# Interleaving two tensors on one core: uniform tile widths and an early output write that is copied from the input in HBM

## The chip, the core and the metric

The kernel runs on one core of a Trainium2 chip. The core has compute engines, of which only VectorE (DVE) computes here, and queues from which transfers are issued: those of SyncE (SP) and ScalarE (ACT). The transfers of both queues run on the same 16 DMA engines. The metric is the device time in microseconds of one execution; the median of several runs is compared. Inputs and output lie in HBM; VectorE works in on-chip memory (SBUF) of 128 partitions.

## What is computed

Two float32 tensors of shape 32 x 256 x 1024 are interleaved element by element into one of 32 x 256 x 2048:

```python
result = np.zeros((batch, seq, dim * 2), dtype=np.float32)
result[..., 0::2] = x
result[..., 1::2] = y
```

67.11 MB are read and 67.11 MB are written, and nothing is calculated.

## The kernel before

All three tensors are taken flat. Each of 128 partitions has 65,536 columns of x and of y in all, cut along the flat tensor into eight tiles whose widths stand in `lwidths` (line 39): 7168, five times 8320, twice 8384. A tile of width `lw` is a block of 128 x `lw` consecutive elements, so the row of one partition begins `lw` elements after that of the partition before, and in the output 2 x `lw` elements after it.

The loop over tiles (line 43) does the following. Line 57 loads x and line 58 loads y, each as one transfer on SP's queue; the x of the first tile is loaded as two halves (line 52), the first on SP's queue and the second on ScalarE's. Then the tile is worked in two halves of width `WS` (lines 68 to 83): VectorE copies x into the even columns of an output tile (line 80) and y into the odd columns (line 81), and the output tile, twice `WS` wide, is written by one transfer on ScalarE's queue (line 82). A row of one partition is contiguous on both sides of each of these transfers.

There are two buffers each of the x tile, the y tile and the output tile. So the load of tile t+2 waits for the copies of tile t, and a copy into an output tile waits for the write that was made of that buffer two halves before. The two queues run independently and the DMA engines serve both.

With the first tile there is an early write (lines 60 to 66): 16 rows of 128 elements of the y tile, 8 KB, are written on ScalarE's queue to where the last tile's output will stand. The values are of no use there; the last tile's own write overwrites them later and waits for the early one to have landed. Since the early write reads the y tile, the load that reuses this buffer, the y of the third tile, waits for it too.

After compilation the order is edited by hand (lines 96 to 115): on each of the two queues the first transfer is taken out of the body and put ahead of the opening barrier, at which all engines meet. In this kernel these two are the halves of the first x tile. At the end (lines 120 to 129) the final wait for the transfers is put on GpSimd (POOL).

Of the kernel before, what the change touches and what calls it, by code (L numbers as in the profile page):

```python
# [3 lines left out]

# [4 lines left out]


@with_exitstack
def _interleave(
    ctx: ExitStack,
    tc: tile.TileContext,
    x: bass.AP,
    y: bass.AP,
    out: bass.AP,
):
    nc = tc.nc  # L20
    P = 128

    total = 1
    for s in x.shape:
        total *= s

    WL = 8384

    xf = x.rearrange("b s d -> (b s d)")
    yf = y.rearrange("b s d -> (b s d)")  # L30
    of = out.rearrange("b s d -> (b s d)")

    fp32 = mybir.dt.float32

    xpool = ctx.enter_context(tc.tile_pool(name="xp", bufs=2))
    ypool = ctx.enter_context(tc.tile_pool(name="yp", bufs=2))
    opool = ctx.enter_context(tc.tile_pool(name="op", bufs=2))

    lwidths = [7168] + [8320] * 5 + [8384] * 2
    assert sum(lwidths) == total // P  # L40

    start = 0
    for lw in lwidths:
        xtile = xpool.tile([P, WL], fp32, name="xtile")[:, :lw]
        ytile = ypool.tile([P, WL], fp32, name="ytile")[:, :lw]

        xs = dataclasses.replace(xf, offset=start, ap=[[lw, P], [1, lw]])
        ys = dataclasses.replace(yf, offset=start, ap=[[lw, P], [1, lw]])
        if start == 0:

            for q, c in ((nc.sync, 0), (nc.scalar, lw // 2)):
                q.dma_start(
                    out=xtile[:, c : c + lw // 2],
                    in_=dataclasses.replace(xf, offset=c, ap=[[lw, P], [1, lw // 2]]),
                )
        else:
            nc.sync.dma_start(out=xtile, in_=xs)
        nc.sync.dma_start(out=ytile, in_=ys)

        if start == 0:  # L60


            early = dataclasses.replace(
                of, offset=2 * (total - P * WL), ap=[[2 * WL, 16], [1, 128]]
            )
            nc.scalar.dma_start(out=early, in_=ytile[:16, :128])

        WS = lw // 2
        soff = 0
        while soff < lw:  # L70
            width = min(WS, lw - soff)
            otile = opool.tile([P, WL], fp32, name="otile")[:, : 2 * width]
            os_ = dataclasses.replace(
                of,
                offset=2 * start + 2 * soff,
                ap=[[2 * lw, P], [1, 2 * width]],
            )
            xsub = xtile[:, soff : soff + width]
            ysub = ytile[:, soff : soff + width]
            nc.vector.tensor_copy(out=otile[:, 0::2], in_=xsub)  # L80
            nc.vector.tensor_copy(out=otile[:, 1::2], in_=ysub)  # L81
            nc.scalar.dma_start(out=os_, in_=otile)
            soff += width

        start += P * lw
    assert start == total


def kernel(tc, x, y, out):
    nc = tc.nc  # L90
    _interleave(tc, x, y, out)
    tc.close()
    tc.compile()  # L93


    blocks = nc.main_func.blocks
    for engine in (mybir.EngineType.SP, mybir.EngineType.Activation):
        opening = blocks[0].instructions
        at, moved = next(
            (b, i)  # L100
            for b in blocks[1:]
            for i in b.instructions
            if i.engine == engine and i.opcode == "DMACopy"
        )
        assert not moved.sync_info.on_wait
        body = at.instructions
        body.remove(moved)
        gate = next(
            n
            for n, i in enumerate(opening)  # L110
            if i.engine == engine and i.opcode == "Drain"
        )
        opening.insert(gate, moved)
        at.instructions = body
        blocks[0].instructions = opening

    last = nc.main_func.blocks[-1]  # L120
    tail = last.instructions
    wait = tail[0]
    clear = next(n for n, i in enumerate(tail) if i.opcode == "ISA")
    assert wait.engine == mybir.EngineType.SP and wait.opcode == "Drain"
    assert wait.sync_info.on_wait and not wait.sync_info.on_update
    assert tail[clear].engine == mybir.EngineType.Pool
    last.instructions = [
        copy.replace(wait, engine=mybir.EngineType.Pool)
    ] + tail[clear:]


# [1 line left out]
_INS = ['x', 'y']  # L133
_OUTS = [((32, 256, 2048), 'float32')]


# [23 lines left out]
```

## Time and profile before

| | |
|---|---|
| median of 5 runs | 315.87 us (315.77 to 316.5) |
| time of the profiled execution | 317.05 us |
| its span in the profile | 315.2 us |
| bytes moved by DMA | 134.23 MB, 426 GB/s over the span |
| VectorE busy | 72.6 us, 32 copies |
| x load of a tile, 4160 KB, issue to landing | 44.3 us |
| y load of a tile, 4160 KB, issue to landing | 61.8 us |
| write of half a tile, 4160 KB, issue to landing | 32.2 us |

The profile is that of one execution. The span runs from the first recorded instruction to the last event; some time of an execution lies around it. The DMA share is the mean busy share of the 16 DMA engines; a transfer is cut into packets that are spread over these engines, and here a packet is one row of a tile. In the timeline SPq and ACTq are the queues' own instructions, which issue transfers; their duration is that of the issue alone. In stretches shorter than a few microseconds the share can exceed 1, because a packet is counted where it begins or ends. Times in the profile are from the start of the span.

### The profile page before, as it was taken

The numbers are of one execution on the slowest core, as the hardware profiler recorded it, in microseconds if no ns is written. First come the engines' busy times: TensorE is split into PE (matmuls) and PEld (weight loads), VectorE is DVE, ScalarE is ACT, GpSimd is POOL, SyncE is SP. The second block draws the span as 40 slices with busy tenths as digits, with TensorE's granted clock in tenths as the row PEclk, the third lists the DMA queues.
The fourth block names the chain that finished last, engine by engine and source line by source line (L and its number), as shares of the span: only waits on it lengthen the run. The fifth ranks groups of instructions, "written<-read, shape, count | busy, mean of one in ns | idle before, by whom it ended". The sixth has DMA issues, their size and how long they took to land.

```text
span 315.2 us, 139 instructions
## 1 busy us (share of the span) xinstructions
DVE 72.6 (23%) x32; POOL 0.2 (0%) x4
## 2 busy tenths in 40 slices
DVE  0540014050220502205022050220502205022500
POOL 0000000000000000000000000000000000000000
DMA  8999999999999999999999999999999999999996
GB/s 347 457 415 411 428 408 436 445 448 427 410 465 414 465 410 427 448 414 465 410 443 431 414 465 414 452 419 416 466 415 445 428 416 468 409 417 468 417 426 260
DMA packets 4784, 134.23 MB, mean 426 GB/s; under 512 B 544, under 2 KB 560, under 8 KB 560
## 3 DMA queue, kind: packets, MB, share of 16 engines
q10 hardware_dynamic: 2480, 68.95, 50.7%
q1 hardware_dynamic: 2304, 65.27, 48.4%
HBM read 67.11 MB, written 67.12 MB: 426 GB/s over the span
## 4 chain that ended last, share of the span: by engine, by line
DMA 83%; DVE 11%; DVEq 1%; issue 0%
DMA out_dram<-otile 77%; DMA ytile<-in_y_dram 6%; DVE otile L81 6%; DVE otile L80 5%; DVEq L93 1%; DVEq L80 0%
## 5 line engine op out<-in xcount | busy, mean ns | idle before, releaser
L80 DVE COPY otile<-xtile 128x4160 f32<-128x4160 f32 (+2 forms) x16 | 36.6, 2294 | 187.7 <-DMA out_dram<-otile 176.9
L81 DVE COPY otile<-ytile 128x4160 f32<-128x4160 f32 (+2 forms) x16 | 36.6, 2291 | 39.3 <-DMA ytile<-in_y_dram 39.3
L144 POOL MEMSET const-bfloat16-1.0<- 128x1 bf16 x1 | 0.1, 101 | 0.0
L144 POOL MEMSET const-uint8-127<- 128x1 uint8 x1 | 0.1, 101 | 0.0
L144 POOL MEMSET const-float32-0.0<- 128x1 f32 x1 | 0.1, 99 | 0.2 <-issue 0.2
L144 POOL MEMSET const-float32-1.0<- 128x1 f32 x1 | 0.1, 98 | 0.0
## 6 DMA issues: line engine op xcount, KB each, us to landing
out_dram<-otile ACTq DMA_DIRECT2D x10, 4160.0 KB, 32.2
xtile<-in_x_dram SPq DMA_DIRECT2D x5, 4160.0 KB, 44.3
ytile<-in_y_dram SPq DMA_DIRECT2D x5, 4160.0 KB, 61.8
out_dram<-otile ACTq DMA_DIRECT2D x4, 4192.0 KB, 21.9
xtile<-in_x_dram SPq DMA_DIRECT2D x2, 4192.0 KB, 44.5
ytile<-in_y_dram SPq DMA_DIRECT2D x2, 4192.0 KB, 62.0
out_dram<-otile ACTq DMA_DIRECT2D x2, 3584.0 KB, 32.6
ytile<-in_y_dram SPq DMA_DIRECT2D x1, 3584.0 KB, 18.8
```

Of the source, the lines that this page charges most:

```text
L80: nc.vector.tensor_copy(out=otile[:, 0::2], in_=xsub)
L81: nc.vector.tensor_copy(out=otile[:, 1::2], in_=ysub)
L93: tc.compile()
L144: nc = _bacc.Bacc("TRN2", target_bir_lowering=False, num_devices=1)
```

## The change

All tiles become 8192 columns wide, and each half 4096; the output tile's buffer is sized to match. The early write is no longer taken from the y tile: the same number of rows and elements, 16 x 128, is copied from the first 16 rows of the x input in HBM to the output in HBM, at the place of the last tile as it now lies. It stands ahead of the loads of the first tile in the program and is ScalarE's first transfer. The hand edit of the order is the same text, and so on ScalarE's queue it now takes this copy ahead of the opening barrier, and the second half of the first x tile stays behind the barrier.

```diff
-    WL = 8384
+    WL = 8192
+    WS = 4096
...
-    lwidths = [7168] + [8320] * 5 + [8384] * 2
+    lwidths = [WL] * (total // P // WL)
...
         if start == 0:
 
+            nc.scalar.dma_start(
+                out=dataclasses.replace(
+                    of, offset=2 * (total - P * WL), ap=[[2 * WL, 16], [1, 128]]
+                ),
+                in_=dataclasses.replace(xf, offset=0, ap=[[WL, 16], [1, 128]]),
+            )
             for q, c in ((nc.sync, 0), (nc.scalar, lw // 2)):
                 q.dma_start(
                     out=xtile[:, c : c + lw // 2],
...
-        if start == 0:
-
-
-            early = dataclasses.replace(
-                of, offset=2 * (total - P * WL), ap=[[2 * WL, 16], [1, 128]]
-            )
-            nc.scalar.dma_start(out=early, in_=ytile[:16, :128])
-
-        WS = lw // 2
         soff = 0
         while soff < lw:
             width = min(WS, lw - soff)
-            otile = opool.tile([P, WL], fp32, name="otile")[:, : 2 * width]
+            otile = opool.tile([P, 2 * WS], fp32, name="otile")[:, : 2 * width]
```

## The prediction, made before the changed kernel was run

> **What bounds the kernel now.** I read the page's summary first, then the chain of waits, then stretches of the span, then the timeline of the opening, and last the trace's records of single DMA packets.
>
> ```profile
> DVE 72.6 (23%) x32; POOL 0.2 (0%) x4
> DMA  8999999999999999999999999999999999999996
> HBM read 67.11 MB, written 67.12 MB: 426 GB/s over the span
> DMA 83%; DVE 11%; DVEq 1%; issue 0%
> ```
>
> VectorE, the only engine that computes, is busy for 23% of the span; the DMA row is full in every slice but the first and the last. The chain of waits gives 11% to VectorE, but that is the chain of one buffer: while a copy runs in it, other transfers are in flight. The stretches show this:
>
> ```profile
> 0.00:1.00 1.00, 0.00 (x0) 0.20 (x4) 1.00 0.05 14
> 1.00:3.00 2.00, 0.00 (x0) 0.00 (x0) 1.00 1.05 323
> 3.00:23.00 20.00, 7.21 (x4) 0.00 (x0) 1.00 1.02 439
> 23.00:27.00 4.00, 0.72 (x1) 0.00 (x0) 1.00 1.04 377
> 27.00:289.00 262.00, 58.08 (x26) 0.00 (x0) 1.00 1.00 433
> 289.00:312.00 23.00, 6.59 (x3) 0.00 (x0) 1.00 0.98 423
> 312.00:315.20 3.20, 0.00 (x0) 0.00 (x0) 1.00 0.03 10
> ```
>
> The last two columns are the DMA share and GB/s. From 27 to 289 us the engines are full at 433 GB/s, with loads alone, writes alone or both. Only four stretches fall short: the first microsecond, 1 to 3 us, 23 to 27 us (377 GB/s while the share stays full, so packets are slow, not missing: (433-377)/433 x 4 = 0.52 us lost), and the end. So what counts is the bytes, the time per packet and the opening and closing; when a single copy or load is issued counts only if both DMA queues ever run dry.
>
> The packet records say the same per engine (16 engines, each with 8 of the 128 rows of a transfer). A packet is one row. Packets of 28672, 33280 and 33536 bytes took 1062, 1232 and 1241 ns: 0.0369 ns per byte and about 4 ns per packet; the 14336-byte rows of the first x load took 533 to 535 where undisturbed. One row of the kernel is 2x533 + 3x1062 for the first tile, 5x4x1232 and 2x4x1241 for the others, 38.82 us, times 8 rows = 310.6 us of the 315.2 us span. On top come a first packet at 1.0 to 1.7 us; packets at 1 to 3 us longer than their size says by 0.61 us per engine; at 23 to 26 us by 0.66; all other excess is 0.16. Successive packets overlap by 3 ns, 0.8 us in all. Fourteen engines end at 312.2 to 312.5, one at 313.1 and the last at 314.3, 0.9 us before the end of the span.
>
> ```profile
> 0.00 0.37 SPq L52 DMA_DIRECT2D xtile<-in_x_dram  x1
> 0.12 0.38 ACTq L52 DMA_DIRECT2D xtile<-in_x_dram  x1
> 0.92 0.33 SPq L58 DMA_DIRECT2D ytile<-in_y_dram  x1
> 19.75 0.35 ACTq L66 DMA_DIRECT2D out_dram<-ytile  x1
> 21.81 2.28 ACTq L82 DMA_DIRECT2D out_dram<-otile  x2
> 25.99 0.33 SPq L58 DMA_DIRECT2D ytile<-in_y_dram  x1
> ...
> SPq L58 <- DMA out_dram<-ytile: 10.9, 1, 10.9
> ...
> out_dram<-ytile ACTq DMA_DIRECT2D x1, 8.0 KB, 6.2
> ```
>
> The early write is issued at 19.75, its sixteen 512-byte packets (27 ns each) run at 23.4 to 24.3 us, and it lands only at 25.95. It is the first write to HBM, and in just this stretch 28 load packets beside it took up to 1986 ns in place of 1232. The first large writes start at 26.7 us and cost next to nothing extra. So the 0.66 us is the price of the first write on each engine, and the early write pays it at 23 us, in the middle of a full queue.
>
> **The change, part by part, against the profiled 315.2 us.**
>
> Widths. Each row becomes 2x609 (16384 bytes) + 3x1213 (32768 bytes) for the first tile and 7x4x1213 for the rest: 38.82 us, times 8 = 310.6. The bytes and the number of packets are the same: 0.00 us. The VectorE copies take some 2.29 us (between 1.98 for 3584 columns and 2.33 for 4160), 73 us in all as before, covered by queued transfers; if both queues ran dry during one pair of copies it would cost 4.6 us. The first tile has 65,536 bytes more per engine to load, 2.4 us, so its y lands at 22.1 instead of 19.7 and the first large write is issued at about 24.5 instead of 21.8. That is hidden: SP has issued x and y of the second tile by 2.6 us, enough for some 39 us of loads from the start. The late writes come out at the end, where ScalarE's queue must not run dry. Before, the last tile's first write is issued at 291.0 and the last one at 299.5, and the write ahead of each lands at 294.8 and some 10 us later, so about 4 and 5 us of slack remain; both shrink by about 1% with the tile, no more. 0.00 us.
>
> One cost of the widths is not in the trace: rows now lie 32,768 bytes apart in x and y and 65,536 in the output, powers of two, in place of 28,672 to 33,536 and 57,344 to 67,072. Bounds: 0 by the rows at 57,344 (7 x 8192), which ran at their nominal 1062 ns; above, the slowed packets of 23 to 26 us are the only rows in which the memory side held up a packet, on average 0.38 us on 28 packets, and if one packet in 32 suffered that it would be 8 x 0.38 = 3.0 us per engine. I take 0, by the nearest pitch.
>
> The Trainium skill speaks against this part: "DMA: Bandwidth & Descriptors", section "Latency and other measured facts", says that rows at large power-of-two distances slow DMA copies and that padding by some KiB restores them; its smallest example, 512 KiB, gives 207 in place of 214 GB/s. By that 3% the sum would be some 10 us higher, 326 us; but 64 KiB is an eighth of its smallest pitch, and no run here shows either.
>
> The early write. Out go its issue at 19.75 and the read of the y tile, and with it the wait of SP's L58 (third y load, behind it nothing for 40 us), which is then released by the last y copy of the first tile at about 26.8 instead of by the landing at 25.95; the x and y loads ahead of it in the queue cover that. In comes a copy from HBM to HBM of sixteen 512-byte rows, the first DMA on ScalarE's queue, issued at 0.12 us. It is 27 ns per engine plus the first-write price. Whether that price goes is the question. At best it falls entirely under the wait for the first loads: -0.66 us. At worst it stays, and the copy's own cold read adds another start like that of the first loads: +0.61. The nearest row is the old early write: beside a full queue it was paid in full, and from 1.0 us on the load queue is full as well. But the first load packets are slow anyway (0.61 us), and a part can lie under these; I take -0.25 us, the part being a guess between 0 and 0.66.
>
> The second half of the first x load. Only the first DMA of each queue is moved ahead of the barrier, and on ScalarE that is now the early copy, so this half goes out behind the barrier, at about 0.95 instead of 0.12 us. Its packets began at 2.5 us before, behind the first ones of SP's half; SP's half alone is 8 x 0.61 = 4.9 us of work per engine, and y is queued behind it, so no engine starves: 0. Without that cover it would cost 0.8 us. Behind it on ScalarE stand only the large writes, which wait for 24 us. VectorE's x copies may start up to 0.8 us later, and had 5.07 us of slack before y. On SP the order is the same; POOL has only the final wait. The last write but one waits for the early copy, landed 290 us before.
>
> Sum: 0.00 + 0.00 - 0.25 = -0.25 us. The profiled execution took 317.05 us around its span of 315.2, and the median of the runs is 315.87, so 1.2 us less; most of that may be the last engine, which ended 1.8 us behind the others. The change is applied to the median: 315.6 us. A profiled span of about 315 follows.
>
> **Rivals.** What a measurement of this kernel can tell from no change is about 0.2%, 0.63 us.
>
> First, the start hides the first write wholly. For it: nothing but 14 GB/s moves in the first microsecond, and the first load packets take 0.85 to 1.5 us, time enough. Against it: load packets and the write wait in the same engine, as at 23 us. Then -0.66, and with any gain on the two engines that end late (they are the two whose first packet comes last, at 1.5 and 1.7 us) about -0.8: 315.1 us.
>
> Second, the other side: the power-of-two pitch slows rows in the steady part. Place: the stretch from 27 to 289 us, where 433 GB/s leaves no cover. Price: 256 packets per engine, so each ns of mean packet time is 0.26 us; it decides from 2.5 ns per packet (1213 to 1215.5). With 8 ns, 2.0 us: 317.9; with the bound of 3.0 us 318.9. For it: no row of the trace has this pitch. Against it: three other pitches run at one rate.
>
> Third, the early copy at the front holds up the first loads: it reads HBM, then writes HBM for the first time, and the engines' loads stand behind it. +0.61 instead of -0.25, and up to 0.3 more through the late second half: about 316.7 us. For it: at 25 us a second load packet in each engine was slow, beside the early write's completion. Against: no load packet before 23 us was.
>
> That the change does not do what it says is ruled out: the order of instructions has the copy as ScalarE's first DMA, ahead of the barrier.
>
> **How the numbers follow.** Forecast (no change that can be told, 315.6): 0.40. Hidden wholly, 315.1: 0.26. Pitch, 317 to 319: 0.19. Held-up start, 316.7: 0.15. Faster by over 0.2% is 0.26, within 0.40, slower 0.34. The forecast's own range is 315.2 to 316.4. The range reaches down to 315.0 for the first rival's better half and up to 317.9, which leaves out the dearer half of the pitch: 315.0 to 317.9, some 2 in 10 outside.
>
> **What would show it.** Right: 32768-byte packets at 1213 ns, 433 GB/s between 27 and 289 us, no dip at 23 to 27 us, a lower rate than 323 GB/s at 1 to 3 us, no gap in both queues near 290. Wrong: a steady rate under 432 (pitch); a dip still at the first large write (the early copy did not pay for it); a first y landing later than 22.8 us (held-up start); or another lag of the last engine, which my sum leaves as it is.

## The result, and the profile after

| | before | changed |
|---|---|---|
| median | 316.3 us (315.57 to 318.4, 55 runs) | 315.57 us (315.34 to 315.9, 29 runs) |
| profiled execution, its span | 317.05, 315.2 us | 315.44, 313.6 us |
| ratio | | 0.997, 95% interval 0.9962 to 0.9978 |

The changed kernel is faster by 0.3% by the ratio; the medians are 0.73 us apart, the means (316.50 and 315.56) 0.94. The five runs shown before the prediction had a median of 315.87; with 55 runs it is 316.3. The lowest runs differ by 0.23 us, the highest by 2.5: what the change took away is mostly the spread upwards. Of the runs before, 14 of 55 stayed below 316 us; of the changed kernel all 29 did.

The same stretches of the changed kernel, with DMA share and GB/s in the last two columns:

```profile
0.00:1.00 1.00, 0.00 (x0) 0.20 (x4) 1.00 0.00 0
1.00:3.00 2.00, 0.00 (x0) 0.00 (x0) 1.00 1.04 311
3.00:23.00 20.00, 5.67 (x3) 0.00 (x0) 1.00 1.03 441
23.00:27.00 4.00, 3.42 (x2) 0.00 (x0) 1.00 0.93 393
27.00:289.00 262.00, 58.21 (x26) 0.00 (x0) 1.00 1.00 432
289.00:312.00 23.00, 5.41 (x3) 0.00 (x0) 1.00 1.00 433
312.00:315.20 3.20, 0.00 (x0) 0.00 (x0) 1.00 0.00 0
```

The long middle is unchanged (433 before, 432 now). The end is not: 433 GB/s between 289 and 312 us where it was 423, and no row of the last write begins after 312 us. The dip at 23 to 27 us has not gone (393, and another 393 from 27 to 31 us); it comes about two microseconds later. The timeline of the opening says with what:

```profile
0.00 0.36 SPq L59 DMA_DIRECT2D xtile<-in_x_dram  x1
0.12 0.59 ACTq L52 DMA_DIRECT2D out_dram<-in_x_dram  x1
...
1.38 0.33 SPq L65 DMA_DIRECT2D ytile<-in_y_dram  x1
1.39 0.37 ACTq L59 DMA_DIRECT2D xtile<-in_x_dram  x1
...
19.50 2.29 DVE L78 COPY otile<-xtile 128x4096 f32<-128x4096 f32 x1 [8.65 <-DMA xtile<-in_x_dram]
...
21.92 4.50 DVE L79 COPY otile<-ytile 128x4096 f32<-128x4096 f32 x2
24.25 2.56 ACTq L80 DMA_DIRECT2D out_dram<-otile  x2
```

The first large write is issued at 24.25 instead of 21.81 us, and the dip follows it. Issuing the copy in HBM takes 0.59 us instead of the 0.38 of the load that stood there, and the loads behind the barrier come 0.46 us later (1.38 instead of 0.92).

The end, closer. First the kernel before, then the changed one:

```profile
305.00:312.00 7.00, 0.00 (x0) 0.00 (x0) 1.00 0.94 407
...
312.60:313.50 0.90, 0.00 (x0) 0.00 (x0) 1.00 0.09 37
```

```profile
305.00:312.00 7.00, 0.00 (x0) 0.00 (x0) 1.00 1.04 449
...
312.60:313.50 0.90, 0.00 (x0) 0.00 (x0) 1.00 0.00 0
```

37 GB/s over 0.9 us are 33 KB, one single row of the last write, begun at 313.03 us: 14 engines have nothing left, a fifteenth ends at 313.08, and the execution waits for one. From the packet records: the last engine ended at 314.27 us before and at 312.64 in the changed kernel, 1.63 us earlier, and the span is shorter by 1.6. The other 14 engines of before end at 312.20 to 312.48, all 16 of the changed kernel at 312.29 to 312.64. So in this pair of executions nearly the whole gain is one engine that no longer comes late. The pair lies 1.6 us apart and the medians 0.73, because the profiled execution of before, 317.05 us, lies that far above its median.

Part of this lateness is made of single load packets that took longer than their size says: by 0.41 us at 31.0 us, 0.05 at 41.6, 0.70 at 43.9, 0.10 at 121.8 and 0.11 at 144.0, 1.37 us in all. The two late engines end 1.88 and 0.69 us behind the median of the 16, some 2.6 us together, so the other 1.2 us are older than that. The records name no engine, but a packet can be joined to the one that begins where it ends, with 8 rows of each transfer to an engine. Read so, the last engine was already 0.73 us behind the median engine at 29 us and took the first three of these packets; the other was 0.49 behind and took the last two. Neither makes it up, since its queue is always full. The changed kernel has no such packet after 29 us, and at 29 us its latest engine is 0.23 us behind.

### The profile page after: what moved, and what is told of

Read it like the earlier page. It is cut to its first block, busy times and chain, and to the rows that moved or that the text cites. A ratio compares the mean times of both kernels' runs of the same rounds, so it can differ in the third digit from the quotient of the medians.

```text
span 313.6 us, 140 instructions
## 1 busy us (share of the span) xinstructions
DVE 72.7 (23%) x32; POOL 0.2 (0%) x4
## 4 chain that ended last, share of the span: by engine, by line
DMA 83%; DVE 11%; DVEq 1%; issue 0%
DMA out_dram<-otile 76%; DMA ytile<-in_y_dram 7%; DVE otile L79 6%; DVE otile L78 5%; DVEq L91 1%; DVEq L78 0%
## 5 line engine op out<-in xcount | busy, mean ns | idle before, releaser
L78 DVE COPY otile<-xtile 128x4096 f32<-128x4096 f32 x16 | 36.7, 2295 | 191.3 <-DMA out_dram<-otile 174.1
L79 DVE COPY otile<-ytile 128x4096 f32<-128x4096 f32 x16 | 36.6, 2292 | 34.3 <-DMA ytile<-in_y_dram 34.1
```

## The experiments

Ratios are to the kernel before, run on the same chip. "Held up" counts load packets after 29 us that took over 25 ns more than their size says; the ends are the first, third last, second last and last of the 16 engines. The table is counted from the packet records of one execution of each:

```
                         held up, longest ns   engines end at (us)
before                        5     702        312.20 .. 312.48 313.08 314.27
e2_early_only                 3     666        312.19 .. 312.69 312.77 313.87
e4_before_no_early            9     517        312.24 .. 312.54 313.37 314.22
e5_8320_first                 0                312.23 .. 312.57 312.80 312.82
e6_narrow_first_8192          4     299        313.60 .. 313.71 313.73 313.79
e7_8064                      25     257        315.65 .. 315.76 315.79 315.81
e8_8448                      17     943        312.26 .. 313.18 313.67 314.01
e9_strided_tiles             64     722        313.20 .. 315.44 315.49 315.59
e11_7168_rows                 3     365        312.36 .. 312.95 312.98 313.29
changed                       0                312.29 .. 312.56 312.57 312.64
e1_widths_only                0                312.27 .. 312.75 312.80 312.81
e3_after_no_early             0                312.34 .. 312.79 312.84 312.96
e10_early_from_sbuf           0                312.29 .. 312.65 312.79 312.85
e12_after_again               0                312.38 .. 312.65 312.71 312.73
```

### Which part of the change: the widths or the opening

**e1: the widths alone.**

```diff
-    WL = 8384
+    WL = 8192
-    lwidths = [7168] + [8320] * 5 + [8384] * 2
+    lwidths = [WL] * (total // P // WL)
```

> The kernel before with eight tiles of 8192 columns and nothing else changed; the early write still reads the y tile. The median of the changed kernel is 315.57 (315.34 to 315.9, all close together), that of before 316.3 (315.57 to 318.4, far apart), and in the profile of before 14 of 16 DMA engines end at 312.2 to 312.5 us, as in the changed kernel, while two end at 313.1 and 314.3. Theory W (the rows of 33280 and 33536 bytes make single engines late): 315.4 to 315.7 with a narrow spread, all engines ending within 0.5 us. Theory E (the early write out of the y tile in the middle of the loads makes single engines late): about 316.3 with a spread of 2 us, one or two engines late. Theory S (what is ahead of the barrier, that is both x halves at once): as theory E, 316.3.

Measured: 315.73 us (315.56 to 316.33, 7 runs), ratio to before 0.9976 (0.9963 to 0.9989). The end of the span:

```profile
305.00:312.00 7.00, 0.00 (x0) 0.00 (x0) 1.00 1.04 449
...
312.60:313.50 0.90, 0.00 (x0) 0.00 (x0) 1.00 0.00 0
```

As theory W had it, with the widths alone the end looks like that of the changed kernel, and no engine is late: they end within 0.54 us. The median is 0.03 us above W's range, and one run of the seven took 316.33.

**e2: the early copy alone.** Before, with the early write taken out behind the y load and put in as:

```diff
+            nc.scalar.dma_start(
+                out=dataclasses.replace(
+                    of, offset=2 * (total - P * WL), ap=[[2 * WL, 16], [1, 128]]
+                ),
+                in_=dataclasses.replace(xf, offset=0, ap=[[lw, 16], [1, 128]]),
+            )
             for q, c in ((nc.sync, 0), (nc.scalar, lw // 2)):
```

> The kernel before, its own widths kept, with the early write copied from x in HBM as ScalarE's first transfer (so the second x half goes behind the barrier). Theory W: 316.3 with a spread of 2 us, since the widths are as before. Theory E: 315.4 to 315.7, narrow. Theory S: 315.4 to 315.7, narrow. In all of them the slow load packets at the first large write, some 0.65 to 0.75 us per engine, stay at about 25 us, if they belong to the first write out of SBUF and not to the first write to HBM.

Measured: 315.94 us (315.78 to 317.08, 12 runs), ratio 0.9981 (0.9971 to 0.9991). The end:

```profile
305.00:312.00 7.00, 0.00 (x0) 0.00 (x0) 1.00 0.99 426
...
312.60:313.50 0.90, 0.00 (x0) 0.00 (x0) 1.00 0.09 37
```

The one late engine is still there, as W expected, and the spread too; but the median is lower than W said, and higher than E and S said. With these widths the opening does count: the early copy alone is faster than before by 0.19%, and 7 of its 12 runs stay below 316 us. By what is not shown, for the profiled execution (316.65 us) took longer than ten of the other eleven runs.

**e3: the changed kernel without any early write.** The copy in HBM is deleted, so the second x half is again ahead of the barrier.

> The changed kernel without any early write: the second x half is again ScalarE's first transfer, ahead of the barrier. Theory W: 315.4 to 315.7, narrow, since the widths decide. Theory E: the same. Theory S: 316.3, wide. If the copy in HBM did pay any of the first write's price, the stall at the first large write is larger than the 0.75 us per engine of the changed kernel; if it paid none, it is the same 0.75 and the time is the changed kernel's within 0.1 us.

Measured: 315.69 us (315.28 to 315.79, 5 runs), ratio 0.9967 (0.9955 to 0.998). Against S, and for W. The slow load packets at the first large write come to 0.86 us per engine without the copy and to 0.67 and 0.79 in two executions with it; e10 below has 0.68. By its own sign the larger 0.86 would mean that the copy pays a part ahead, but e4 below, without any early write, has 0.65, so 0.1 to 0.2 us is within what varies between single executions. Most of the price is not paid ahead.

**e4: the kernel before without any early write.** Its lines 60 to 66 are deleted.

> The kernel before without any early write, its own widths kept. Theory W: 316.3, wide. Theory E: 315.4 to 315.7, narrow, since the early write out of the y tile is gone. Theory S: 316.3, wide. The stall at the first write moves from 23 to 26 us to the first large write, at about the same 0.66 us per engine.

Measured: 316.23 us (315.69 to 316.97, 12 runs), ratio 0.9991 (0.9979 to 1.0002).

```profile
23.00:27.00 4.00, 0.92 (x1) 0.00 (x0) 1.00 1.02 375
...
312.60:313.50 0.90, 0.00 (x0) 0.00 (x0) 1.00 0.09 37
```

Two engines end late, at 313.37 and 314.22 us, and the spread is wide, as W said. E falls: the early write out of the y tile is gone and the lateness stays. And the dip between 23 and 27 us is there without any early write, 375 GB/s against 377 in the kernel before. It belongs to the first large write. e3 and e4 differ in the widths alone (and in the buffers' size with them): 315.69 against 316.23.

By time alone the two parts are not cleanly separated: the interval of e2, the early copy alone, overlaps that of e1, the widths alone, and those of e3 and e4 touch. The spread and the records separate them. Of the 65 runs of the five kernels with 8192 columns in consecutive blocks (changed 29, e1 7, e3 5, and e10 and e12 below with 12 each) 63 stay below 316 us; of the 79 runs with the old widths (before 55, e2 12, e4 12) 26 do. None of the five traces of the first kind has a load packet held up, all three of the second have. These three traces are of executions well above their medians (317.05, 316.65 and 316.93 us); what one below 316 us looks like with the old widths was not seen.

### What in the widths

**e5 to e8: four sets of widths in e4.** `WL`, the width of the buffers, goes with the widest tile.

```diff
-    lwidths = [7168] + [8320] * 5 + [8384] * 2
+    lwidths = [8320] * 7 + [7296]
...
+    lwidths = [7168] + [8192] * 6 + [4608] * 2
...
+    lwidths = [8064] * 8 + [1024]
...
+    lwidths = [8448] * 7 + [6400]
```

> No early write; seven tiles of 8320 columns and the narrow one (7296) last. Rows of 33280 bytes, which are over 32 KiB, 65 x 512 bytes, no power of two. An engine is called late if it ends more than 0.5 us after the bulk (312.2 to 312.8 us in all runs so far). Theory N (a narrow first tile makes an engine late): none late, 315.5 to 315.8 with a narrow spread. Theory L (rows over 32 KiB): one or two late by 0.5 to 1.9 us, 315.9 to 316.7, wide. Theory G (rows that are an odd multiple of 512 bytes): late, as L. Theory P (rows whose distance is no power of two): late, as L.

> No early write; a first tile of 7168 columns, then six of 8192 and two of 4608: no row over 32 KiB, all multiples of 1 KiB. Two more transfers of each kind than eight tiles have, and a shorter tail. Theory N: one or two engines late by 0.5 to 1.9 us, wide. Theories L and G: none late, a narrow spread, 315.4 to 316.0. Theory P: between, since most rows are 32 KiB apart.

> No early write; eight tiles of 8064 columns and one of 1024. Rows of 32256 bytes: under 32 KiB, 63 x 512 bytes, no power of two. Theory N: none late. Theory L: none late, 315.4 to 316.2 (nine tiles). Theory G: late by 0.5 to 1.9 us, wide. Theory P: late, wide.

> No early write; seven tiles of 8448 columns and one of 6400. Rows of 33792 bytes: over 32 KiB, 33 KiB exactly, no power of two. Theory N: none late. Theory L: late by 0.5 to 1.9 us, wide, 315.9 to 316.7. Theory G: none late. Theory P: late, wide.

Measured: e5 315.98 us (315.52 to 316.07), ratio 0.9979 (0.9965 to 0.9993); e6 317.2 (316.94 to 318.18), 1.0022 (1.0003 to 1.0042); e7 318.18 (318.0 to 319.25), 1.0052 (1.0033 to 1.0071); e8 316.31 (315.85 to 320.14), 1.0004 (0.9975 to 1.0033). None of the four theories passes all four. N falls: e8 has no narrow first tile, and two of its engines end over 0.5 us after the bulk. L is weakened by e6 and e7, which have no row over 32 KiB and still have held-up packets, 4 and 25, though short ones and with no engine late at the end. G falls with e8, 33 KiB exactly. P says held-up packets wherever rows are not a power of two, and meets e5, whose profiled execution has none. That execution was the fastest of its ten (315.52; the other nine 315.76 to 316.07), so what the others had is not seen. By its time e5, with rows of 8320 columns and the narrow tile last, cannot be told from e1 (0.9979 and 0.9976). The width of the buffers is not the cause by itself: e6, and e11 and e9 below, have buffers of 8192 columns and held-up packets.

e6 and e7 cannot be read by their time: their engines end within 0.2 us of each other, but late together, because the small tiles at the end let the queues run dry. e7:

```profile
305.00:312.00 7.00, 0.43 (x1) 0.00 (x0) 1.00 0.88 374
...
312.60:313.50 0.90, 0.76 (x2) 0.00 (x0) 1.00 0.07 27
313.50:316.00 2.50, 0.00 (x0) 0.00 (x0) 1.00 0.52 210
```

VectorE makes its last two copies while 27 GB/s move; the last write is issued behind them. In such a hole a late engine can catch up, which would explain the common end.

**e11: rows of 28 KiB.** `lwidths = [7168] * 8 + [8192]` and `WL = 8192`, else e4.

> No early write; eight tiles of 7168 columns and one of 8192 last. Rows of 28,672 bytes, which are 7 x 4 KiB and no power of two. Nine tiles, so 32 more packets per engine at about 1 ns each. Theory K (what counts is that rows begin on 4 KiB boundaries): no load packet held up after the first writes, all engines within 0.7 us of each other, 315.6 to 316.0, narrow. Theory P (what counts is a power of two): single packets held up by 0.1 to 0.9 us after 29 us, wide.

Measured: 316.68 us (316.38 to 317.39, 12 runs), ratio 1.0002 (0.999 to 1.0014). Three packets held up, by 0.37, 0.16 and 0.14 us, and the engines end 0.93 us apart: K fails, and P's size is at its lower end.

**e9: the same rows, further apart.** In e3, a tile becomes a block of columns of the flat tensors seen as 128 x 65536:

```diff
-        xs = dataclasses.replace(xf, offset=start, ap=[[lw, P], [1, lw]])
+        xs = dataclasses.replace(xf, offset=start // P, ap=[[total // P, P], [1, lw]])
...
-                offset=2 * start + 2 * soff,
-                ap=[[2 * lw, P], [1, 2 * width]],
+                offset=2 * start // P + 2 * soff,
+                ap=[[2 * total // P, P], [1, 2 * width]],
```

> No early write, eight tiles of 8192 columns, but a tile takes a column block of the 128 x 65536 view instead of a consecutive block: rows of x and y lie 262,144 bytes apart and rows of the output 524,288, with the same runs of 32 KiB and the same packets. Theory A (large power-of-two distances hold up packets, the second rival of the prediction): packets over 1213 ns in the steady part, a rate below 432 GB/s, up to some 325 us. Theory B (32 KiB runs alone decide): 1213 ns, no packet held up after 29 us, 315.5 to 315.8 as without the early write on consecutive blocks (315.69).

Measured: 317.68 us (316.79 to 318.29, 10 runs), ratio 1.0039 (1.0023 to 1.0055).

```profile
31.00:289.00 258.00, 56.82 (x25) 0.00 (x0) 1.00 1.00 432
...
305.00:312.00 7.00, 0.00 (x0) 0.00 (x0) 1.00 0.94 407
...
313.50:316.00 2.50, 0.00 (x0) 0.00 (x0) 1.00 0.09 39
```

64 load packets held up, and four engines end at 314.7 to 315.6. Theory B fails: runs of 32 KiB alone do not protect. A was right in kind and far off in size: 317.68 against 315.69 is 2.0 us or 0.6%, while the median packet is still 1213 ns and the middle still moves 432 GB/s. The cost is single packets on single engines again.

**Where the held-up packets fall.** Joined to engines as above, the three traces with the old widths (before, e2, e4) have all their 17 held-up packets on engines that were already 0.43 us or more behind the median engine. At 29 us the latest engine of these traces is 0.73, 0.52 and 1.01 us behind; in the five traces with 8192 columns in consecutive blocks it is 0.20 to 0.43. So lateness begins in the opening and grows later. It does not always grow: e5 has an engine 0.45 us behind and no packet held up. And in e8 three long ones, 0.73 to 0.94 us, fall at 29.5 to 29.8 us on engines that were ahead. Whether the widths keep the engines in step during the opening, or spare an engine that is out of step afterwards, no experiment separates.

### Can the first write's price be hidden

**e10: an early write out of SBUF.** In e3, behind the first loads:

```diff
+        if start == 0:
+            etile = epool.tile([16, 128], fp32, name="etile")
+            nc.vector.memset(etile, 0.0)
+            nc.scalar.dma_start(
+                out=dataclasses.replace(
+                    of, offset=2 * (total - P * WL), ap=[[2 * WL, 16], [1, 128]]
+                ),
+                in_=etile,
+            )
```

> The changed kernel with its early copy in HBM taken out, and in its place an early write of the same place out of a small SBUF tile that VectorE fills with zeros; it waits for no load and goes out right behind the barrier, behind the x half. Theory F (the slow load packets at 25 to 28 us, 0.67 us per engine, belong to the first write out of SBUF, wherever it comes): they move to the first 5 us and are gone at 25 to 28 us. If the slow start (0.66 us there already) covers them, 315.0 to 315.3; if they add up, 315.5 to 315.8. Theory H (they belong to the first large write): they stay at 25 to 28 us, 315.6.

Measured: 315.62 us (315.45 to 316.18, 12 runs), ratio 0.9974 (0.9961 to 0.9986).

```profile
1.00:3.00 2.00, 0.17 (x1) 0.00 (x0) 1.00 1.02 303
...
23.00:27.00 4.00, 3.65 (x2) 0.00 (x0) 1.00 0.94 393
27.00:31.00 4.00, 0.00 (x0) 0.00 (x0) 1.00 1.05 393
```

The dip stays in its place, at 0.68 us per engine: H. The small write did not run in the first 5 us, though, but behind the x half at 13.8 to 14.5 us, in the middle of full queues like the early write of before, and no load packet beside it was slow: between 5 and 22 us the excess is below 0.02 us per engine. In every kernel the first slow load packet follows the issue of the first large write by 1.1 to 1.7 us (before: 21.81 and 23.4; changed: 24.25 and 25.9; e4: 22.02 and 23.4), whatever small write came ahead. Whether a large write at the very front would hide the price was not tried.

**e12: the changed kernel again**, beside e9 to e11.

> The changed kernel again, beside the three others: 315.4 to 315.7, narrow, no load packet held up after 29 us, all engines ending within 0.5 us.

Measured: 315.54 us (315.39 to 315.8, 12 runs), ratio 0.9967 (0.9956 to 0.9979), as expected. No experiment gave a version that beats the changed kernel.

## Why the prediction was right and wrong

The time, 315.57 us, is the forecast 315.6 almost to the digit, and inside the range; that is luck, as the steps show. But the forecast called it no change that can be told, and it is faster by 0.22 to 0.38%; the case "faster", at 0.26, came true, and by another mechanism than the one written under it. Two of the signs that the prediction named for being wrong appeared: the dip at the first large write, and another lag of the last engine. By its steps:

- **Equal bytes, equal packets, 0.00 us.** Right. 32768-byte packets took 1213 ns, the middle moves 432 GB/s, and the bulk of the engines ends within 0.2 us of where it did.
- **Copies of 2.29 us, y at 22.1, first write at 24.5, no dry queue.** Right: 2.29 and 2.30 us, 21.90, 24.25, and the write issue at the end was in time.
- **The pitch, taken as 0 with a loss as the only other end.** Wrong, and this is the step that failed. I looked for harm in the new distances only and took the median packet of the old ones as proof that they did none. The widths of before are the ones in which packets were held up; e1 alone brought 0.9976. The lag of the last engine stood in my own ledger (314.3 against 312.5) and in the sum as a constant: "another lag of the last engine, which my sum leaves as it is". In the profiled pair it is the one term that the change moved clearly, by 1.63 us. The last engine of before did begin late, at 1.7 us, as the prediction has it, but that was not enough: one in the changed kernel began at 1.94 and ended at 312.53.
- **The early write, -0.25 us, as part of a first-write price of 0.66.** Wrong. The price is that of the first large write: e4 pays 0.65 with no early write at all, e10 0.68 with one from SBUF, the changed kernel 0.67. I read the cause from what happened at the same time; the large write had been issued 1.6 us ahead of the dip too. With uniform widths the kind of early write makes at most 0.2 us between medians (315.54 to 315.73), less than the spread of these runs. And the copy in HBM did not run at the front: issued at 0.12, its packets ran at 4.7 to 5.2 us.
- **The second x half, 0.8 us later, hidden.** Hidden, but mis-sized: it was not 0.8 us late but about 7. Behind the early copy its last packet ended at 17.9 us (10.9 before), and VectorE finished copying it at 21.79, 0.13 us before it turned to y. In e10, with that half ahead of the barrier, both copies were done at 16.3. A little more would have been on VectorE's path, though not yet on that of the DMA engines.
- **The power-of-two rival, 0.19.** It did not happen at 32 and 64 KiB; e9 has it at 256 and 512 KiB at 0.6%. "DMA: Bandwidth & Descriptors" of the Trainium skill, section "Latency and other measured facts", has 207 in place of 214 GB/s for 512 KiB, 3% less, and advises to pad the rows or to lay the tiles out contiguously. Here the measured 0.6% decides, for reads at 256 KiB and writes at 512. The padded rows of before, with their narrow first tile, are slower than the unpadded ones of e1 by 0.24%; those of e5, without it, cannot be told from them.
- **The held-up start, 0.15.** Load packets up to 5 us ran over by 0.66 us per engine, 0.64 before: it did not happen.
- **The base.** Applying -0.25 to the median of five put the forecast at 315.6; applied to 316.3 it would have been 316.05. Two errors met: the gain was too small by 0.5 us, and the base by 0.4.

What stays open is the cause: why no load packet is held up with rows of 8192 columns in consecutive blocks (five kernels or repeats, five traces) where it happens in nearly all other layouts, and how far the lateness that an engine brings from the opening decides it. Row length, narrow first tile, 512-byte multiples, 4 KiB multiples and 32 KiB runs were each tried and none alone explains it. Open too is why, with the old widths, the opening of e2 has the lower median (0.9981, where e4 has 0.9991; the intervals overlap).

## What to carry to other kernels

Where all DMA engines are full from end to end, the time is that of the last engine, not of the mean: look at when each engine ends. A spread between runs can have its cause there. A median packet at its nominal duration doesn't show that a layout is harmless; count the few packets that ran over. Before a stall is charged to the small transfer beside it, take that transfer out.

## What was not expected

- A copy of 8 KB inside HBM, first in its queue, took 6.0 us from issue to landing, and the load half queued behind it began its packets at 6.0 us, where it had begun at 2.5 us from the front of the queue.
- The first large write makes load packets slow by 0.6 to 0.9 us per engine, once, in all the layouts of consecutive blocks (1.06 in e9), and its own first packet runs 4.9 us after its issue in the kernel before and in the changed one.
- Kernels with nine tiles (e6, e7, e11) have 2.2 us of their time outside the span, those with eight 1.8 to 1.9.
